# Attention heads of an encoder block: squaring before splitting, scores before q's low part, and small softmax steps on GpSimd

## The chip, the cores and the metric

The kernel runs on one core of a Trainium2 chip. A core has five engines that work side by side and are tied together by semaphores: TensorE (PE in the profile; its weight loads are PEld), VectorE (DVE), ScalarE (ACT), GpSimd (POOL) and SyncE (SP), which here only issues DMAs. Each engine takes its instructions strictly in the order in which the kernel gives them. The metric is the device time of one execution in microseconds (us). Before the change the median of three runs is 946.17 us (945.48 to 946.81).

## The reference

One layer of a bidirectional encoder on 256 tokens of width 2048, in float32:

```python
h = _rmsnorm(x, norm1_g)
proj = h @ w_in                      # q (12 heads x 128) | k, v (4 x 128 each) | u (512)
a = _rmsnorm(_window_attention(q, k, v, sink), attn_out_g)
f = _rmsnorm(_fourier_mix(u, w_fourier), fourier_out_g)
x = x + jnp.concatenate([a, f], axis=-1) @ w_out
x = x + _conv_ffn(_rmsnorm(x, norm2_g), w_up, dw_w, dw_b, w_down)
return _rmsnorm(x, normf_g)
```

Three query heads share one key and value head. The attention of one head, with the parts that the change touches:

```python
scores = einsum(q, k) * HEAD_DIM ** -0.5 - slope * |t - s|      # NEG_INF beyond 128
m = maximum(max(scores), sink)
p = exp(scores - m)
p = p / (sum(p) + exp(sink - m))
out = einsum(p, v)
```

The RMS norm over all heads' outputs needs the sum of their squares.

## The kernel before

**Products in three parts.** Every float32 operand of a matmul is split into a high part (`hi`, the value rounded to the matmul's reduced format) and a low part (`lo`, the rest). A product is hi x hi + lo x hi + hi x lo. ACT makes the high part by a copy (line 181 for weights, line 269 in `split_scaled`), DVE the low part by a subtraction (lines 182 and 270), so the low part always waits for the high one.

**Units.** The weights come in 1 MB units of 128 x 2048. `unit(i, work)` issues, in this order: the steps registered for `before` unit i, the matmuls of the unit, the steps registered `beside` it, the split of the weights of unit i + 2 (ACT `hi`, 1.9 us, then DVE `lo`, 2.3 us), and the steps `behind`. Units 0 to 3 are the projection u, 4 to 7 v, 8 to 23 the four groups k, q, q, q (line 350), 24 to 39 the output projection (lines 333 to 335). From 256 us on comes the feed-forward part, which the change leaves alone.

**A head's way through the units.** The order is written out by hand in the loop over `N_QK` to `N_OUT + 8`. For a q head computed in unit s:

- s + 1, beside: `qk_out` (ACT copies one half of the product out of PSUM as `tmp_q`, DVE adds the other: `add_q`; for k, DVE multiplies by r1b as well, line 635) and `qk_parts` (ACT writes the high part of `qT`, DVE the low part).
- s + 2, before: `scores`, six matmuls on `qT` and `kT` (line 654). For either token block the first two need only `qT`'s high part, the third needs the low part. Beside: `scores_out`, on DVE two fused add-and-maximum passes (line 670), then two instructions of 128 x 2 (lines 674 and 675) that give `neg`, the negated maximum. Behind: `exps`, on ACT, which needs `neg`.
- s + 3, beside: `weigh`, on DVE: the sum `sm` (line 693), its reciprocal (694), two scalings of the probabilities in place (697), and `flip_out`, a block transpose (314) whose result SP sends through memory.
- s + 6, beside: `flip_parts` (lines 739 and 740) splits the transposed probabilities.
- s + 7, before: `values`, six matmuls (line 749); beside: `values_out`, that is `feature_out`: `split_scaled` on the head's output in PSUM (ACT, then DVE), then the square on ACT (line 486 for the first head, 489 for the others), and for all but the first head an addition to `sq_a` on GpSimd (line 490).

The last two heads take a shorter way with a transpose on TensorE. `feature_out` also serves the four Fourier groups, whose outputs lie in SBUF. PSUM is read by one engine at a time: where ACT and DVE both read one tile of PSUM, the second waits for the first, so the square of a head's output waits for DVE's `cat` (line 270).

The pattern repeats every four units. Units 8, 12, 16, 20 compute k. In a unit that follows a k unit (17, 21) the new slot is k; in units 10, 14, 18, 22 there are no scores to take out; in units 11, 15, 19, 23 there is no `weigh` and no `values`.

**Buffers that matter here.** `hi` and `lo` have three buffers each, so a split runs up to two units ahead of its matmuls. `qT`, `mx`, `neg`, `sm` and `ex` have two each, the square's scratch `junk` one.

Of the kernel before, what the change touches and what calls it, by code (L numbers as in the profile page):

```python
# [8 lines left out]
F32 = mybir.dt.float32  # L9
F32R = mybir.dt.float32r  # L10
AF = mybir.ActivationFunctionType
ALU = mybir.AluOpType

P = 128
D = 2048
S = 256
# [88 lines left out]
def block_kernel(  # L105
# [19 lines left out]
    nc = tc.nc  # L125
# [3 lines left out]
    wp = ctx.enter_context(tc.tile_pool(name="wp", bufs=1))  # L129
# [3 lines left out]
    def f32(ap):  # L133
        return ap.bitcast(F32)

    def bank(pool, name):
        return pool.tile([P, 512], F32, tag=pool.name, name=name)
# [79 lines left out]
    def u_part(k, o, n, m=1):  # L217

        rows = ux[k // 4][:, (k < 4) * U_HEAD :].rearrange("p (k c) -> p k c", k=4)
        return rows[:, k % 4 : k % 4 + m, o : o + n]  # L220
# [39 lines left out]
    ps = bank(dn, "ps_warm")  # L260
# [3 lines left out]
    def vcol(o, n=1):  # L264
        return vec[:, o : o + n]

    def split_scaled(dst, src, g):

        nc.scalar.activation(dst[:, 0:S], src, AF.Copy, scale=g)
        nc.vector.scalar_tensor_tensor(  # L270
            dst[:, S : 2 * S], src, g, f32(dst[:, 0:S]), ALU.mult, ALU.subtract
        )
# [100 lines left out]
    before, beside, behind = {}, {}, {}  # L373

    def at(when, i, f, *a):
        when.setdefault(i, []).append((f, a))
# [17 lines left out]
    for k in range(NK):  # L394
# [7 lines left out]
        if q % n == 0:  # L402
            w, h = u_part(k, 0, FW, n), hi[:, q : q + n, :]
# [26 lines left out]
    rq_neg = ph.tile([P, 2], F32, tag="rq_neg", name="rq_neg")  # L430
    rq_pos = ph.tile([P, 2], F32, tag="rq_pos", name="rq_pos")
    rq_inv = ph.tile([P, 2], F32, tag="rq_inv", name="rq_inv")
    sink_neg = ph.tile([P, NH], F32, tag="sink_neg", name="sink_neg")
# [46 lines left out]
    def feature_out(ps, slot, g, sq, first):  # L480

        t = cat_pool.tile([P, 512], F32R, tag="cat", name=f"cat{slot}")
        split_scaled(t, ps, g)
        cat[slot] = t
        if first:
            nc.scalar.activation(sq, ps, AF.Square)
        else:
            one = wp.tile([P, 512], F32, tag="junk", name=f"sq{slot}")[:, 0:S]
            nc.scalar.activation(one, ps, AF.Square)
            nc.gpsimd.tensor_tensor(sq, sq, one, ALU.add)  # L490

    sums, r_af = {}, {}
# [91 lines left out]
    def fourier_channels_out(g):  # L584
        feature_out(held.pop(("y", g)), NH + g, vcol(V_GF + g), sq_f, g == 0)
# [43 lines left out]
    def qk_out(kind, h, ps):  # L629
        tmp = ph.tile([P, S], F32, tag="tmp", name=f"tmp_{kind}{h}", bufs=2)  # L630
        nc.scalar.activation(tmp, ps[:, S : 2 * S], AF.Copy)
        add = ph.tile([P, S], F32, tag="add", name=f"add_{kind}{h}", bufs=2)
        nc.vector.tensor_tensor(add, ps[:, 0:S], tmp, ALU.add)
        if kind == "k":
            nc.vector.tensor_tensor(add, add, r1b, ALU.mult)
        st["add", kind, h] = add
# [25 lines left out]
    def scores_out(h):  # L662

        ps = st.pop(("s", h))
        sc = ph.tile([P, 512], F32, tag="sc", name=f"sc{h}", bufs=4)
        mx = ph.tile([P, 2], F32, tag="mx", name=f"mx{h}", bufs=2)
        neg = ph.tile([P, 2], F32, tag="neg", name=f"neg{h}", bufs=2)
        for b in range(2):
            s = slice(b * S, (b + 1) * S)
            nc.vector.tensor_tensor_reduce(  # L670
                sc[:, s], ps[:, s], rel[:, s], -float(SL[h]), -3e38, ALU.add,
                ALU.max, mx[:, b : b + 1],
            )
        nc.vector.tensor_tensor(neg, mx, rq_neg, ALU.mult)
        nc.vector.tensor_scalar(neg, neg, sink_neg[:, h : h + 1], None, ALU.min)
        st["sc", h] = sc, neg

    def exps(h):
        sc, neg = st["sc", h]
        sm = ph.tile([P, 2], F32, tag="sm", name=f"sm{h}", bufs=2)  # L680
        ex = ph.tile([P, 2], F32, tag="ex", name=f"ex{h}", bufs=2)
        for b in range(2):
            s = slice(b * S, (b + 1) * S)
            nc.scalar.activation(
                sc[:, s], sc[:, s], AF.Exp, scale=rq_pos[:, b : b + 1],
                bias=neg[:, b : b + 1], accum_out=sm[:, b : b + 1],
            )
        nc.scalar.activation(ex, neg, AF.Exp, bias=vcol(V_SINK + h))
        st["sc", h] = sc, sm, ex

    def weigh(h):
        sc, sm, ex = st["sc", h]
        nc.vector.tensor_tensor(sm, sm, ex, ALU.add)
        nc.vector.reciprocal(ex, sm)
        for b in range(2):
            s = slice(b * S, (b + 1) * S)
            nc.vector.tensor_scalar(sc[:, s], sc[:, s], ex[:, b : b + 1], None, ALU.mult)
# [59 lines left out]
    def values_out(h):  # L757
        feature_out(st.pop(("o", h))[:, 0:S], h, vcol(V_GA + h), sq_a, h == 0)
# [3 lines left out]
    for i in range(N_QK, N_OUT + 8):  # L762
        heads = {i - s: h for (kind, h), s in slot_of.items() if kind == "q"}
        new = [kh for kh, s in slot_of.items() if i - s == 1]
        for n, h in sorted(heads.items()):
            if n == 5 + 2 * (h in FLIPS):
                at(before, i, values, h)
        if 4 in heads and heads[4] not in FLIPS:
            at(before, i, turn, heads[4])
        if 2 in heads:  # L770
            at(before, i, scores, heads[2])
        if 6 in heads and heads[6] in FLIPS:
            at(beside, i, flip_parts, heads[6])
        if 3 in heads:
            at(beside, i, weigh, heads[3])
            if heads[3] in FLIPS:
                at(beside, i, flip_out, heads[3])
        if 4 in heads and heads[4] in FLIPS:
            at(beside, i, flip_in, heads[4])
        for kind, h in new:  # L780
            at(beside, i, lambda k=kind, h=h: qk_out(k, h, st.pop(("ps", k, h))))
        for n, h in sorted(heads.items()):
            if n == 5 + 2 * (h in FLIPS):
                at(beside, i, values_out, h)
        if 4 in heads and heads[4] not in FLIPS:
            at(beside, i, turn_out, heads[4])
        for kind, h in new:
            at(beside, i, qk_parts, kind, h)
        if 2 in heads:
            at(beside, i, scores_out, heads[2])  # L790
            at(behind, i, exps, heads[2])

    fourier_channels_steps()
# [84 lines left out]
    for n, (c, kq) in enumerate(OUT_ORDER):  # L878
        i = N_OUT + n
# [14 lines left out]
        if kq >= 2:  # L894
            part = "a" if kq == 2 else "f"
            ps = ps_a[c] if kq < 3 else ps_a[c, "f"]
# [315 lines left out]
    for q in range(2):  # L1212
        kind, j = items[q]
        ps = bank(mm, f"ps_{kind}{j}")
# [15 lines left out]
    for n, it in enumerate(items):  # L1230
# [8 lines left out]
        if it[0] in ("gate", "val"):  # L1239
            kind, j = it  # L1240
            ps = bank(mm, f"ps_{kind}{j}")
# [4 lines left out]
        if it[0] == "product":  # L1246
# [4 lines left out]
            elif end and p in ("P2", "N4"):  # L1251
                ps = joined[c, p] = bank(mm, f"ps_{p}{g}{c}")
                by_parts(ps, parts[p], *halves.pop(it), GROUPS[g][1], True, False)
            else:
                ps = bank(mm, f"ps_{p}{g}{c}")
# [5 lines left out]
        else:  # L1261
            kind, c = it
            hi, lo = halves.pop(up_index[n])
            if c < 2:
                ps = [joined.pop((c, p)) for p in ("P2", "N4")]
            else:
                ps = [bank(mm, f"ps_l{c}{b}") for b in range(2)]
# [10 lines left out]
    i = up_index[n]  # L1278
# [37 lines left out]
    junk = wp.tile([P, 512], F32, tag="junk", name="junkc31")[:, 0:256]  # L1316
# [120 lines left out]
```

## Time and profile before

| what | value |
|---|---|
| median of three runs | 946.17 us (945.48 to 946.81) |
| the profiled execution | 944.83 us, of which the span is 943.0 us |
| TensorE busy | 930.6 us, 99% of the span |
| VectorE busy | 771.4 us, 82% |
| ScalarE busy | 540.5 us, 57% |
| GpSimd busy | 50.8 us, 5%, 68 instructions |
| mean granted TensorE clock | 0.993 |

Times in the profile are microseconds from the start of the span. A line of a timeline gives the start, the duration, the engine, the line of the kernel, the operation, and output <- inputs; what stands in brackets is the idle time of the engine before it and what ended that. Matmuls overlap, so a line's duration is longer than its distance to the next. The profiled execution is 1.34 us shorter than the median.

### The profile page before, as it was taken

How to read it: one execution, taken by the hardware profiler on the slowest of the kernel's cores; microseconds unless marked ns; L12 is line 12 of the kernel's file. 1: busy time of each engine (PE TensorE's matmuls, PEld its weight loads, DVE VectorE, ACT ScalarE, POOL GpSimd, SP SyncE). 2: the span in 40 equal slices, each digit the busy share in tenths (PEclk: the TensorE clock that was granted, in tenths of full speed). 3: DMA queues.
4: the chain of work that ended last, by engine and by line, in shares of the span. 5: the costliest groups of instructions: out<-in, count | busy, mean ns of one | idle time of the engine just before them, and what ended most of it. 6: DMA issues, size and time to landing. Idle time of an engine off the chain costs nothing.

```text
span 943.0 us, 12851 instructions
## 1 busy us (share of the span) xinstructions
PE 930.6 (99%) x5005; PEld 805.6 (85%) x5005; DVE 771.4 (82%) x981; ACT 540.5 (57%) x672; POOL 50.8 (5%) x68
## 2 busy tenths in 40 slices
PE   9999989999999999999999999999999999999996
PEld 7888878888888888888888888888888888888885
DVE  7658788777777878799887997878988779989986
ACT  7755566645554564566555565555655556655553
POOL 0100000100000000000000000000000000000002
PEclk9999989999999999999999999999999999999998
DMA  9965766566766578877798769787787878779652
GB/s 364 310 224 168 225 200 190 191 209 248 259 229 206 183 238 245 269 250 235 250 272 254 243 230 284 241 265 228 260 247 239 301 240 266 226 236 277 201 179 89
DMA packets 55149, 223.26 MB, mean 237 GB/s; under 512 B 21136, under 2 KB 25744, under 8 KB 31536
## 3 DMA queue, kind: packets, MB, share of 16 engines
q1 hardware_dynamic: 50544, 192.94, 56.6%
q0 software_dynamic: 4544, 29.49, 16.7%
q8 instruction: 39, 0.64, 0.3%
q14 instruction: 22, 0.18, 0.1%
HBM read 216.13 MB, written 6.29 MB: 236 GB/s over the span
## 4 chain that ended last, share of the span: by engine, by line
PE 88%; DVE 5%; ACT 4%; issue 2%; DMA 1%; DVEq 0%; SPq 0%; POOLq 0%; POOL 0%; ACTq 0%
PE ps_val L350 25%; PE ps_gate L350 25%; PE ps_P L1148 3%; PE ps_P L1146 3%; PE ps_P L1147 3%; PE ps_N L1148 3%; PE ps_N L1147 3%; PE ps_N L1146 3%; PE ps_a L335 2%; PE ps_a L334 2%; PE ps_a L333 2%; ACT hi L181 2%; DVE lo L182 1%; PE ps_ff L333 1%; PE ps_ff L335 1%
## 5 line engine op out<-in xcount | busy, mean ns | idle before, releaser
L182 DVE TENSOR_TENSOR lo<-raw,hi 128x2048 fp32r<-128x2048 f32 (+1 forms) x129 | 293.4, 2274 | 46.4 <-ACT hi L181 43.7
L181 ACT ACTIVATE hi<-raw 128x2048 fp32r<-128x2048 f32 (+1 forms) x129 | 245.2, 1901 | 34.2 <-PE ps_a L334 14.4
L350 PE MATMUL ps_val<-hU,hi 128*128 128x512 f32 x688 | 236.2, 389 | 0.0
L350 PE MATMUL ps_gate<-hU,hi 128*128 128x512 f32 x688 | 236.2, 389 | 0.0
L350 PE MATMUL ps_val<-hU,lo 128*128 128x256 f32 x688 | 189.9, 276 | 0.0
L350 PE MATMUL ps_gate<-hU,lo 128*128 128x256 f32 x688 | 189.9, 276 | 0.0
L350 PEld LDWEIGHTS ps_gate<-hU,hi 128*128 128x128 f32 x688 | 129.2, 188 | 26.8
L350 PEld LDWEIGHTS ps_val<-hU,hi 128*128 128x128 f32 x688 | 129.1, 188 | 26.8
L350 PEld LDWEIGHTS ps_gate<-hU,lo 128*128 128x128 f32 x688 | 129.2, 188 | 1.3
L350 PEld LDWEIGHTS ps_val<-hU,lo 128*128 128x128 f32 x688 | 129.2, 188 | 1.3
L921 ACT ACTIVATE ft_g<-ps_gate 128x256 f32<-128x256 f32 x43 | 16.5, 384 | 123.1 <-PE ps_gate L350 123.1
L921 ACT ACTIVATE ft_v<-ps_val 128x256 f32<-128x256 f32 x43 | 16.5, 384 | 91.8 <-PE ps_val L350 91.8
L350 PE MATMUL ps_q<-hT,hi 128*128 128x512 f32 x192 | 67.2, 401 | 0.0
L1146 PE MATMUL ps_P<-hi_P,op_P 128*128 128x512 f32 x144 | 56.0, 389 | 0.0
L1147 PE MATMUL ps_P<-hi_P,op_P 128*128 128x512 f32 x144 | 56.0, 389 | 0.0
L1148 PE MATMUL ps_P<-lo_P,op_P 128*128 128x512 f32 x144 | 56.0, 389 | 0.0
L350 PE MATMUL ps_q<-hT,lo 128*128 128x256 f32 x192 | 52.0, 281 | 0.0
L1038 DVE TENSOR_TENSOR lo_N<-sumw,hi_N 128x2048 fp32r<-128x2048 f32 (+1 forms) x20 | 41.5, 2076 | 9.4 <-ACT hi_N L1037 9.2
L350 PEld LDWEIGHTS ps_q<-hT,hi 128*128 128x128 f32 x192 | 36.3, 194 | 7.0
L1146 PE MATMUL ps_N<-hi_N,op_N 128*128 128x512 f32 x108 | 42.0, 389 | 0.0
L1147 PE MATMUL ps_N<-hi_N,op_N 128*128 128x512 f32 x108 | 42.0, 389 | 0.0
L1148 PE MATMUL ps_N<-lo_N,op_N 128*128 128x512 f32 x108 | 42.0, 389 | 0.0
(389 smaller groups left out, 1584.7 us busy)
## 6 DMA issues: line engine op xcount, KB each, us to landing
raw<-in_w_up SPq DMA_DIRECT2D x86, 1024.0 KB, 5.6
raw<-in_w_in SPq DMA_DIRECT2D x20, 1024.0 KB, 5.2
raw<-in_w_out SPq DMA_DIRECT2D x16, 1024.0 KB, 5.0
sumw<-in_w_down POOLq DMA_DIRECT2D x16, 1024.0 KB, 8.7
raw<-in_w_down_late SPq DMA_DIRECT2D x4, 1024.0 KB, 6.9
raw<-in_w_down_last SPq DMA_DIRECT2D x4, 768.0 KB, 4.2
turnp<-flip SPq DMA_DIRECT2D x40, 64.0 KB, 3.0
flop<-turnp SPq DMA_DIRECT2D x10, 256.0 KB, 4.0
```

The costliest lines, as they stand in the source:

```text
L181: nc.scalar.activation(hi[:, 0:n], raw[:, 0:n], AF.Copy)
L182: nc.vector.tensor_tensor(lo[:, 0:n], raw[:, 0:n], f32(hi[:, 0:n]), ALU.subtract)
L333: nc.tensor.matmul(ps, ah, wh, start=first and q == q0, stop=False)
L334: nc.tensor.matmul(ps, al, wh, start=False, stop=False)
L335: nc.tensor.matmul(ps, ah, wl, start=False, stop=last and q == q0 + len(kk) - 1)
L350: nc.tensor.matmul(ps[:, x], (hi, lo)[i][:, k * P : (k + 1) * P], hk(k)[:, x], start=n == 0 and k == 0, stop=n == len(order) - 1 and k == ...
L921: nc.scalar.activation(tmp, ps[:, S : 2 * S], AF.Copy)
L1038: nc.vector.tensor_tensor(lo, src, f32(hi), ALU.subtract)
L1146: nc.tensor.matmul(ps, o[:, 0, p, :], hi[:, s], start=first and p == 0, stop=False)
L1147: nc.tensor.matmul(ps, o[:, 1, p, :], hi[:, s], start=False, stop=False)
L1148: nc.tensor.matmul(ps, o[:, 0, p, :], lo[:, s], start=False, stop=last and p == n - 1)
```

## The change

Three edits.

1. In `feature_out` ACT squares the head's output before it is split, so on ACT the square stands ahead of the high part of `cat`, and it no longer comes after DVE's low part.
2. In each unit `scores_out` is registered ahead of `qk_parts`, so on DVE the two passes of line 670 stand ahead of the low part of the new `qT` or `kT`.
3. Three instructions of 128 x 2 per head move from DVE to GpSimd: lines 674 and 675 (`neg`), and the sum of line 693, which now stands in `exps`, behind the exponentials. `exps` now waits for GpSimd, and the reciprocal of `weigh` as well.

```diff
     def feature_out(ps, slot, g, sq, first):
 
         t = cat_pool.tile([P, 512], F32R, tag="cat", name=f"cat{slot}")
+        one = sq
+        if not first:
+            one = wp.tile([P, 512], F32, tag="junk", name=f"sq{slot}")[:, 0:S]
+        nc.scalar.activation(one, ps, AF.Square)
         split_scaled(t, ps, g)
         cat[slot] = t
-        if first:
-            nc.scalar.activation(sq, ps, AF.Square)
-        else:
-            one = wp.tile([P, 512], F32, tag="junk", name=f"sq{slot}")[:, 0:S]
-            nc.scalar.activation(one, ps, AF.Square)
+        if not first:
             nc.gpsimd.tensor_tensor(sq, sq, one, ALU.add)
...
-        nc.vector.tensor_tensor(neg, mx, rq_neg, ALU.mult)
-        nc.vector.tensor_scalar(neg, neg, sink_neg[:, h : h + 1], None, ALU.min)
+        nc.gpsimd.tensor_tensor(neg, mx, rq_neg, ALU.mult)
+        nc.gpsimd.tensor_scalar(neg, neg, sink_neg[:, h : h + 1], None, ALU.min)
         st["sc", h] = sc, neg
...
         nc.scalar.activation(ex, neg, AF.Exp, bias=vcol(V_SINK + h))
+        nc.gpsimd.tensor_tensor(sm, sm, ex, ALU.add)
         st["sc", h] = sc, sm, ex
...
         sc, sm, ex = st["sc", h]
-        nc.vector.tensor_tensor(sm, sm, ex, ALU.add)
         nc.vector.reciprocal(ex, sm)
...
+        if 2 in heads:
+            at(beside, i, scores_out, heads[2])
         for kind, h in new:
             at(beside, i, qk_parts, kind, h)
         if 2 in heads:
-            at(beside, i, scores_out, heads[2])
             at(behind, i, exps, heads[2])
```

On GpSimd the order of a unit is then: the addition of line 490, the two instructions of `neg`, and, behind the exponentials, the sum. All else keeps its order on every engine; the DMA queues are as before.

## The prediction

> **What bounds the kernel now.** The page first: TensorE is busy for 99% of the span, so a change on other engines can only give back what TensorE waits, and what it loses after a wait. The view of waits, for PE alone, says where that is.
>
> ```profile
> PE 930.6 (99%) x5005; PEld 805.6 (85%) x5005; DVE 771.4 (82%) x981; ACT 540.5 (57%) x672; POOL 50.8 (5%) x68
> ```
>
> ```profile
> PE ps_s L654 <- ACT qT L269: 2.5, 1, 2.5
> ...
> PE ps_s L654 <- DVE qT L270: 0.2, 1, 0.2
> ```
>
> Both waits are scores that come before their q is split. PE's timeline places them: at the start of units 19 and 23.
>
> ```profile
> 95.91 1.20 PE L654 MATMUL ps_s<-kT,qT 128*128 128x256 f32 x6
> ...
> 122.15 0.40 PE L350 MATMUL ps_q<-hT,lo 128*128 128x256 f32 x2
> 125.09 2.01 PE L654 MATMUL ps_s<-kT,qT 128*128 128x256 f32 x6 [2.54 <-ACT qT L269]
> ...
> 134.56 0.40 PE L749 MATMUL ps_o<-pt,v_hi 128*128 128x256 f32 x2
> ...
> 148.34 0.40 PE L749 MATMUL ps_o<-pt,v_hi 128*128 128x256 f32 x2
> ...
> 149.06 0.63 PE L350 MATMUL ps_q<-hT,hi 128*128 128x512 f32 x2
> ...
> 154.54 0.40 PE L654 MATMUL ps_s<-kT,qT 128*128 128x256 f32 x2
> 155.15 0.74 PE L654 MATMUL ps_s<-kT,qT 128*128 128x256 f32 x4 [0.22 <-DVE qT L270]
> 155.74 0.63 PE L350 MATMUL ps_q<-hT,hi 128*128 128x512 f32 x2
> ```
>
> A unit's 32 matmuls take 5.48 us (149.06 to 154.54); units 20 to 22 with all that stands between take 19.98 us (134.56 to 154.54) without a wait. The wait at unit 19 costs more than its 2.54 us, as windows around it show (last columns: granted clock, DMA share, GB/s):
>
> ```profile
> 121.30:124.70 3.40, 1.25 (x8) 0.93 (x7) 2.85 (x8) 0.94 (x4) 0.00 (x0) 1.00 0.50 149
> 124.73:128.15 3.42, 3.06 (x10) 2.59 (x11) 2.03 (x2) 2.99 (x6) 0.72 (x1) 0.50 0.95 300
> 128.15:131.56 3.41, 3.41 (x12) 2.86 (x11) 2.93 (x8) 1.36 (x2) 0.00 (x0) 0.50 0.36 98
> ```
>
> From 124.73 us, 2.18 us after PE fell idle (122.15 + 0.40), until 131.56 the clock is at half: work from 125.09 to 131.56 goes half as fast, which costs 3.24 us. In all unit 19 is some 6 us late. Yet not all of that can be won: by 154 us PE has run into the next wait. The pace there is set by a loop between ACT and DVE, read from their timelines for unit 18 (DVE, then ACT, whose last line is the same step of unit 22):
>
> ```profile
> 118.47 0.41 DVE L670 CUSTOM_DVE_ANT_0 sc<-ps_s,rel 128x256 f32<-128x256 f32 x1
> ...
> 119.27 0.16 DVE L674 TENSOR_TENSOR neg<-mx,rq_neg 128x2 f32<-128x2 f32 x1
> 119.46 0.23 DVE L675 TENSOR_SCALAR neg<-neg,sink_neg 128x2 f32<-128x2 f32 x1
> 119.60 2.29 DVE L182 TENSOR_TENSOR lo<-raw,hi 128x2048 fp32r<-128x2048 f32 x1
> 121.80 0.15 DVE L693 TENSOR_TENSOR sm<-sm,ex 128x2 f32<-128x2 f32 x1
> 121.99 0.17 DVE L694 RECIPROCAL ex<-sm 128x2 f32<-128x2 f32 x1
> 122.19 0.62 DVE L697 TENSOR_SCALAR sc<-sc,ex 128x256 f32<-128x256 f32 x2
> 122.84 0.71 DVE L314 STREAM_TRANSPOSE flip<-sc 128x512 f32<-128x512 f32 x1
> 123.48 0.39 DVE L633 TENSOR_TENSOR add_q<-ps_q,tmp_q 128x256 f32<-128x256 f32 x1
> 123.79 0.47 DVE L270 SCALAR_TENSOR_TENSOR cat<-ps_o,vec,cat 128x256 fp32r<-128x256 f32 x1
> 125.07 0.75 DVE L270 SCALAR_TENSOR_TENSOR qT<-add_q,qT 128x256 fp32r<-128x256 f32 x1 [0.81 <-ACT qT L269]
> ```
>
> ```profile
> 117.65 1.91 ACT L181 ACTIVATE hi<-raw 128x2048 fp32r<-128x2048 f32 x1
> 119.79 0.60 ACT L684 ACTIVATE sc<-sc,neg,rq_pos 128x256 f32<-128x256 f32 x1 [0.23 <-DVE neg L675]
> ...
> 121.16 0.36 ACT L631 ACTIVATE tmp_q<-ps_q 128x256 f32<-128x256 f32 x1
> 121.43 0.46 ACT L269 ACTIVATE cat<-ps_o,vec 128x256 fp32r<-128x256 f32 x1
> 124.35 0.39 ACT L489 ACTIVATE sq<-ps_o 128x256 f32<-128x256 f32 x1 [2.46 <-DVE cat L270]
> 124.63 0.41 ACT L269 ACTIVATE qT<-add_q 128x256 fp32r<-128x256 f32 x1
> 124.94 1.90 ACT L181 ACTIVATE hi<-raw 128x2048 fp32r<-128x2048 f32 x1
> ...
> 154.20 1.91 ACT L181 ACTIVATE hi<-raw 128x2048 fp32r<-128x2048 f32 x1
> ```
>
> Loop: ACT's hi at 117.65, DVE's lo, weigh, flip, add_q, cat, then ACT's sq, qT and the next hi at 124.94. It takes 7.29 us here, and from unit 18 to unit 22 it takes 29.26 us (154.20 − 124.94), where PE's four units would take about 26.2 (19.98 + 5.48 + 0.72 for unit 19 without a wait; 0.72 is values, 148.34 to 149.06, and scores take about the same). So PE gains on the loop by 3 us in every group and meets it at units 19 and 23. After unit 23 PE waits no more, so what is won there stays to the end.
>
> **The change part by part.**
>
> *Square ahead of the split.* The view of waits shows what goes:
>
> ```profile
> ACT sq L489 <- DVE cat L270: 24.9, 11, 3.3
> ```
>
> Unit 18: add_q ends at 123.87, yet qT starts at 124.63, because sq waits for cat's low part. Now sq stands at 121.43, behind tmp_q and ahead of cat's high part, in time in which ACT idled 2.46 us; qT can start at 123.90. That takes 0.73 us off the loop, in each of the units 16, 17, 18, 20, 21, 22 that holds a head's output and precedes the waits. In the Fourier groups the square also comes first, and DVE's cat waits some 0.4 us longer; DVE idles longer than that for the next hi, so this costs nothing:
>
> ```profile
> 70.00 2.29 DVE L182 TENSOR_TENSOR lo<-raw,hi 128x2048 fp32r<-128x2048 f32 x1 [1.89 <-ACT hi L181]
> ```
>
> *Line 490 on GpSimd comes earlier with it,* and what it meets changes.
>
> ```profile
> 124.81 0.72 POOL L490 TENSOR_TENSOR sq_a<-sq_a,sq 128x256 f32<-128x256 f32 x1 [6.55 <-ACT sq L489]
> ```
>
> ```profile
> 130.65 0.42 DVE L270 SCALAR_TENSOR_TENSOR qT<-add_q,qT 128x256 fp32r<-128x256 f32 x1 [0.48 <-ACT qT L269]
> ```
>
> The qT step that begins at 125.07 beside this addition takes 0.75 instead of 0.42 us, and ends 0.29 us after the addition does: DVE was held. There it delays scores, not the loop. After the change the addition is ready at 121.82, while DVE's lo runs, and would lie at about 122.0 to 122.74, beside the reciprocal and the scaling of line 697. No row shows whether that scaling is held. If not: 0. If held until the addition ends, it finishes at about 122.9 instead of 122.5, or 0.35 us later; a subtraction of line 740 in its place (units 17, 20, 21) could lose 0.6. I take 0.33, nearest the row that shows a hold. The Trainium skill, page "SBUF — State Buffer", section "Who interferes with whom", says that DVE's two-input and two-port instructions and GpSimd exclude each other for a whole instruction, whichever comes first blocking the other, and counts tensor_scalar among those that can take two ports. The row above agrees for GpSimd coming first; by this rule the 0.33 is due, and the gain of the first edit nearly halves.
>
> *Three small steps to GpSimd.* DVE loses 0.20 + 0.14 (119.27 to 119.60) and 0.19 us (121.80). The first two were beside ACT's hi and gain little. GpSimd's nearest rows: 0.19 us for a small addition, 0.70 for a power.
>
> ```profile
> L280 POOL TENSOR_TENSOR rstda<-vara,half_pow 128x2 f32<-128x2 f32 x1 | 0.7, 702 | 7.3 <-DVE vara L277 7.3
> ...
> L1323 POOL TENSOR_TENSOR ssq<-ssq 128x1 f32<-128x1 f32 x2 | 0.4, 192 | 1.2 <-ACT junkc L1165 0.9 <-ACT junkc L1317 0.3
> ```
>
> I take 0.2 each. sm is ready once the exponentials end at 121.16. If GpSimd runs it at once, the reciprocal follows lo directly: −0.19. If lo holds it until 121.80, sm ends at 122.0 and the reciprocal stays where it was, at worst 0.05 later. I take 0, and +0.1 for the heads before unit 15, where no head's output is there to gain on: the scores at 95.91 start 0.1 us later. For neg, the exponentials must not wait: priced as a rival.
>
> *Scores ahead of qT's low part.* DVE fills its idle 0.81 us before qT's low part with four instructions of 0.80 us (118.47 to 119.27). Behind them waits the low part, which the third score matmul needs: against the loop it ends up to 0.4 us later in units 16, 20 and 24, so the scores of the unit after could come to wait; the bounds are 0 and 0.4 each, 0.8 ahead of unit 23. Units 18 and 22, which feed the two waits, hold no scores_out, so I take 0. No DMA and no queue is moved.
>
> *Sum.* Loop starts of hi: unit 18 at 124.94 + 0.1 − 0.73 (unit 16, whose first head adds nothing on GpSimd) − 2 × 0.40 = 123.5. PE, at 122.65, finds qT's high part at 123.6: it waits 0.9 us instead of 2.54, too short, I take it, for the clock to fall. Unit 22's hi: 154.20 + 0.1 − 0.73 − 5 × 0.40 = 151.6. In unit 23 before, q's matmuls began 1.54 us after that hi, of which 0.33 was a hold of qT by the addition, as at 125.07, that is now gone: 152.8 against 155.74, 2.95 us earlier. PE itself arrives in time: unit 19 ends at 123.5 + 1.2 + 5.48 = 130.2, unit 22 at 150.2, so it waits about 1.4 us at unit 23, again without a fall. I round to 3.0 us: 944.83 − 3.0 = 941.8 for an execution like the profiled one, which was 1.34 below the median, so **943.2** as a median.
>
> **The rivals.**
>
> *The clock falls at the wait of unit 23.* PE is ahead of the loop now, and the wait grows from 0.22 us, at which the clock stayed, to 1.4; before, 2.18 us idle sufficed. A fall costs what it cost then, 3.24 us, and takes the gain: 944.83 − 3.0 + 3.2 = 945.0, 946.4 as a median. (A fall at unit 19 instead would mostly be absorbed at unit 23: PE would arrive there 3.24 later, 153.4, plus 0.7 for scores, so gain 1.6.) The Trainium skill, "TensorE: Matmul & The Clock Gate", Part 1, lets the clock fall after a window of about 3.4 us of idling; by that neither wait would do it, but here 2.18 us did, so the row decides.
>
> *Nothing holds anything.* Six units save 0.73 + 0.19: hi of unit 22 at 148.7, PE no longer waits at unit 19 nor, to speak of, at 23, and of its losses of 6.0 and 0.5 some 6 come back: 944.83 − 6.0 = 938.8, median 940.2.
>
> *The holds eat it.* 0.6 for line 740, 0.05 for sm and an added 0.1 leave nothing: 946.2.
>
> *Slower: neg falls behind the split's lo.* The passes of line 670 now end about 0.78 us after ACT's hi begins (add_q to hi 0.73; cat 0.31 + 0.40 and 0.80 after add_q), qT's low part 0.34 later, and DVE's lo begins 1.95 after it (117.65 to 119.60). Held behind qT, the two GpSimd steps start at 1.12 and need 0.4 to 0.5: done by 1.6, slack 0.35. At 0.70 each they still get in, the second at 1.85, and lo loses 0.5. If the second starts after 1.95 and lo holds it to 4.15, the exponentials (1.37 us, 119.79 to 121.16) end at 5.8, the reciprocal moves from 4.34 to 6.0, 1.65 us per unit. Six units: 9.9 lost against 3.0, 944.83 + 6.9 = 951.7, median 953.1.
>
> **How the numbers follow.** Chances: the forecast 0.48 (own range 941.5 to 944.5), the clock falls 0.20, nothing holds 0.12, holds eat it 0.10, slower 0.10. The range 940.2 to 947.6 takes in the free case, the fallen clock and the eaten gain, and leaves out the last. This kernel can tell 0.2%, 1.9 us, from no change: faster means below 944.3, the forecast almost wholly and the free case, 0.57 with the forecast's upper edge taken off; within are the fallen clock, the eaten gain and that edge, 0.31; slower 0.12, the last case and a clock that falls at both waits.
>
> **What would show it.** Right: no wait of sq on cat; qT 0.03 us behind add_q; unit 19's wait near 0.9 us at full clock, unit 23's near 1.4; scalings of line 697 longer than 0.35 us beside line 490; line 689 held until lo ends; exponentials directly behind hi. Wrong: half clock near 150 us; neg later than lo's start; PE's waits elsewhere than at units 19 and 23.

## The result, and the profile after

The changed kernel takes 941.28 us (median; 940.97 to 941.60) against 946.39 us (945.48 to 946.81) for the kernel before in the same comparison. The ratio is 0.995, with a 95% interval of 0.9936 to 0.9964: faster by 0.54%. In a second comparison (the last row of the table below) the ratio was 0.9955 (0.9943 to 0.9967). The forecast was a gain of 3.0 us to 943.2; the gain is 5.1 us in the first comparison and 4.0 in the second. The profiled executions, 944.83 and 941.03 us, differ by 3.8.

The page's line of busy times and the view of PE's waits, of the changed kernel:

```profile
PE 928.0 (99%) x5005; PEld 803.5 (86%) x5005; DVE 765.5 (82%) x945; ACT 539.6 (57%) x672; POOL 72.9 (8%) x104
```

```profile
PE ps_s L654 <- ACT qT L269: 1.4, 2, 0.9
```

The two waits lie where they lay before, at the starts of units 19 and 23 (PE's timeline of the changed kernel; the last row is the start of q's matmuls of unit 23):

```profile
122.94 1.19 PE L654 MATMUL ps_s<-kT,qT 128*128 128x256 f32 x6 [0.54 <-ACT qT L269]
...
150.43 1.20 PE L654 MATMUL ps_s<-kT,qT 128*128 128x256 f32 x6 [0.85 <-ACT qT L269]
151.47 0.61 PE L350 MATMUL ps_q<-hT,hi 128*128 128x512 f32 x2
```

They were 2.54 and 0.22 us. q's matmuls of unit 23 start at 151.47 instead of 155.74 us. The table by windows gives the same from PE's side: busy time of each engine from 110 to 160 us, then granted clock, DMA share and GB/s, first of the kernel before, then of the changed one:

```profile
110.00:160.00 50.00, 47.24 (x273) 41.78 (x272) 41.42 (x93) 30.51 (x67) 3.68 (x5) 0.93 0.63 187
```

```profile
110.00:160.00 50.00, 48.60 (x299) 43.16 (x298) 41.15 (x79) 32.76 (x76) 12.91 (x21) 1.00 0.69 210
```

In the same 50 us PE issues 26 more matmuls: it is busy for 1.36 us more, as its waits are shorter, and the clock stays full (1.00 instead of 0.93). The view of waits has no row of sq on cat any more. This is the loop of unit 18 in the changed kernel, DVE, ACT and GpSimd, to be held against the timelines in the prediction:

```profile
117.93 2.29 DVE L182 TENSOR_TENSOR lo<-raw,hi 128x2048 fp32r<-128x2048 f32 x1 [0.87 <-ACT hi L181]
120.31 0.17 DVE L694 RECIPROCAL ex<-sm 128x2 f32<-128x2 f32 x1
120.51 0.86 DVE L697 TENSOR_SCALAR sc<-sc,ex 128x256 f32<-128x256 f32 x2
121.41 0.71 DVE L314 STREAM_TRANSPOSE flip<-sc 128x512 f32<-128x512 f32 x1
122.05 0.39 DVE L633 TENSOR_TENSOR add_q<-ps_q,tmp_q 128x256 f32<-128x256 f32 x1
```

```profile
116.00 1.90 ACT L181 ACTIVATE hi<-raw 128x2048 fp32r<-128x2048 f32 x1
...
119.42 0.37 ACT L486 ACTIVATE sq<-ps_o 128x256 f32<-128x256 f32 x1
119.69 0.46 ACT L269 ACTIVATE cat<-ps_o,vec 128x256 fp32r<-128x256 f32 x1
122.47 0.42 ACT L269 ACTIVATE qT<-add_q 128x256 fp32r<-128x256 f32 x1 [2.32 <-DVE add_q L633]
122.79 1.90 ACT L181 ACTIVATE hi<-raw 128x2048 fp32r<-128x2048 f32 x1
```

```profile
116.80 0.31 POOL L674 TENSOR_TENSOR neg<-mx,rq_neg 128x2 f32<-128x2 f32 x1 [3.09 <-DVE mx L670]
117.21 0.28 POOL L675 TENSOR_SCALAR neg<-neg,sink_neg 128x2 f32<-128x2 f32 x1
119.33 0.94 POOL L689 TENSOR_TENSOR sm<-sm,ex 128x2 f32<-128x2 f32 x1 [1.84 <-ACT ex L688]
120.24 0.72 POOL L490 TENSOR_TENSOR sq_a<-sq_a,sq 128x256 f32<-128x256 f32 x1
```

The loop takes 6.79 us (116.00 to 122.79) where it took 7.29. From add_q to the next hi it is 0.74 instead of 1.46 us, the square's 0.72. From the reciprocal to the flip it is 1.10 instead of 0.85, since the scaling pair takes 0.86 instead of 0.62 beside line 490. GpSimd's sum of 128 x 2, line 689, takes 0.94 us: it ends at 120.27, 0.05 after DVE's lo, so the reciprocal starts 2.38 us behind lo's start, as before (2.39).

In units 16, 17, 20 and 21, DVE's line 740 stands between lo and the reciprocal, and there the sum does pay. Unit 17, DVE of the kernel before, then of the changed one:

```profile
111.17 2.29 DVE L182 TENSOR_TENSOR lo<-raw,hi 128x2048 fp32r<-128x2048 f32 x1 [0.24 <-ACT hi L181]
113.38 0.76 DVE L740 TENSOR_TENSOR pt<-flop,pt 128x256 fp32r<-128x256 f32 x2
114.05 0.15 DVE L693 TENSOR_TENSOR sm<-sm,ex 128x2 f32<-128x2 f32 x1
114.24 0.17 DVE L694 RECIPROCAL ex<-sm 128x2 f32<-128x2 f32 x1
```

```profile
110.15 2.30 DVE L182 TENSOR_TENSOR lo<-raw,hi 128x2048 fp32r<-128x2048 f32 x1 [0.88 <-ACT hi L181]
112.36 0.76 DVE L740 TENSOR_TENSOR pt<-flop,pt 128x256 fp32r<-128x256 f32 x2
113.03 0.16 DVE L694 RECIPROCAL ex<-sm 128x2 f32<-128x2 f32 x1
113.23 0.90 DVE L697 TENSOR_SCALAR sc<-sc,ex 128x256 f32<-128x256 f32 x2
```

Lo's start to the reciprocal: 3.07 before, 2.88 after, all of the sum's 0.19. Line 740 itself is not held (0.76 both times).

### The profile page after: what moved, and what is told of

It reads as the page before. It is cut to its first block, busy times and chain, and to the rows that moved or that the text cites. A ratio compares the mean times of both kernels' runs of the same rounds, so it can differ in the third digit from the quotient of the medians.

```text
span 938.9 us, 12849 instructions
## 1 busy us (share of the span) xinstructions
PE 928.0 (99%) x5005; PEld 803.5 (86%) x5005; DVE 765.5 (82%) x945; ACT 539.6 (57%) x672; POOL 72.9 (8%) x104
## 4 chain that ended last, share of the span: by engine, by line
PE 95%; DVE 2%; ACT 1%; issue 1%; DMA 0%; POOL 0%; DVEq 0%; POOLq 0%; ACTq 0%
PE ps_val L350 25%; PE ps_gate L350 25%; PE ps_q L350 5%; PE ps_P L1148 3%; PE ps_P L1149 3%; PE ps_P L1147 3%; PE ps_N L1148 3%; PE ps_N L1149 3%; PE ps_N L1147 3%; PE ps_k L350 2%; PE ps_a L333 2%; PE ps_a L335 2%; PE ps_a L334 2%; PE ps_s L654 1%; PE ps_ff L333 1%; PE ps_ff L335 1%
## 5 line engine op out<-in xcount | busy, mean ns | idle before, releaser
L350 PE MATMUL ps_q<-hT,hi 128*128 128x512 f32 x192 | 65.1, 391 | 0.0
```

Source lines behind the costliest of these rows:

```text
L350: nc.tensor.matmul(ps[:, x], (hi, lo)[i][:, k * P : (k + 1) * P], hk(k)[:, x], start=n == 0 and k == 0, stop=n == len(order) - 1 and k == ...
```

## The experiments

The theory after the comparison: the time follows the ACT and DVE loop of units 16 to 22, and each edit counts by what it takes from that loop; the square gives, the addition on GpSimd takes some of it back, and the scores' place does nothing. Rivals: the gain is the full clock alone; or it is the 0.5 us per head that DVE no longer does.

**The kernel before, again.** 

> The kernel before, unchanged, for a second profile. Is the length of the half clock after the wait of unit 19 fixed? If the clock is looked at in windows of 3.41 us that run freely (6.83 us of half clock in the first profile are two of them), the start of the half clock relative to the wait differs here, and its length is a whole number of 3.41 us; the time of the execution goes with it by 1.7 us per window. If the length is fixed by the wait, start and length repeat within 0.1 us. Time 945.5 to 946.8 us.

945.59 us beside 945.64, ratio 0.9998 (0.9989 to 1.0007). Its profiled execution (945.78 us) has the half clock for 3.4 us only (126.16 to 129.57 us), not the 6.83 of the execution that the prediction used. It starts 2.93 us after PE fell idle instead of 2.18, so start and length are not fixed by the wait, as expected of free windows. That the time goes with it by 1.7 us did not come: from unit 15's hi to the first matmul of the output projection it is 61.28 us here (102.03 to 163.31) and 61.30 in the other execution (101.34 to 162.64). So the loop, not the clock, set the time: what the clock leaves at unit 19, PE waits at unit 23, as the prediction said in brackets. There the wait for qT's high part is 0.93 us, where the other execution waited 0.22 us in all:

```profile
155.05 0.50 PE L654 MATMUL ps_s<-kT,qT 128*128 128x256 f32 x2 [0.93 <-ACT qT L269]
```

**The first edit alone.**

```diff
+        one = sq
+        if not first:
+            one = wp.tile([P, 512], F32, tag="junk", name=f"sq{slot}")[:, 0:S]
+        nc.scalar.activation(one, ps, AF.Square)
         split_scaled(t, ps, g)
         cat[slot] = t
-        if first:
-            nc.scalar.activation(sq, ps, AF.Square)
-        else:
...
+        if not first:
             nc.gpsimd.tensor_tensor(sq, sq, one, ALU.add)
```

> The first edit alone: the square ahead of the split, all else as before. Loop theory (what counts is the time from one ACT hi to the next in units 16 to 22, because PE meets that loop at units 19 and 23): each of six units loses 0.73 us of waiting and, beside line 490, gets back about 0.28 us of a held scaling (none in unit 16): hi of unit 22 at 154.20 - 0.73 - 5 x 0.45 = 151.2, about 3 us less in all, 943 to 943.5 us; no half clock at unit 19. Load theory (what counts is work taken off VectorE): no VectorE instruction goes, so 946 us, no change.

943.29 us, ratio 0.9976 (0.9966 to 0.9985): the time is in the expected range, with 2.35 us gained where about 3 was expected. The way there was not as expected, so the range was met in part by luck: from unit 15 to unit 22 the loop gave 1.55 us (52.86 to 51.31 between the hi's), not 2.98. Unit 18's gave 0.19 us, not 0.73 less a small hold: the sum of line 693, still on DVE, is now held by GpSimd's addition (GpSimd's timeline, then DVE's, then a window around unit 19):

```profile
120.60 0.94 POOL L490 TENSOR_TENSOR sq_a<-sq_a,sq 128x256 f32<-128x256 f32 x1 [6.62 <-ACT sq L486]
```

```profile
120.88 0.69 DVE L693 TENSOR_TENSOR sm<-sm,ex 128x2 f32<-128x2 f32 x1
...
121.81 0.61 DVE L697 TENSOR_SCALAR sc<-sc,ex 128x256 f32<-128x256 f32 x2
```

```profile
124.80:128.20 3.40, 3.40 (x14) 2.91 (x13) 2.44 (x2) 1.81 (x4) 0.00 (x0) 0.50 0.73 183
```

0.69 us for an instruction that took 0.15: 0.54 of the 0.73 is lost there. And no half clock was expected, yet the clock fell after a wait of 1.55 us.

**The second edit alone.**

```diff
+        if 2 in heads:
+            at(beside, i, scores_out, heads[2])
         for kind, h in new:
             at(beside, i, qk_parts, kind, h)
         if 2 in heads:
-            at(beside, i, scores_out, heads[2])
             at(behind, i, exps, heads[2])
```

> The second edit alone: lines 670 to 675 ahead of the low part of qT or kT on VectorE, all else as before. Loop theory: DVE's next lo waits for ACT's hi in any case, and hi waits for sq and qT, which do not move: no change, 945.5 to 946.8 us, the stall of unit 19 as before with half clock. Load theory: 0.8 us of VectorE's idle time is filled in nine units, some 3 us or more less: 943 us.

945.28 us, ratio 0.9999 (0.999 to 1.0008): nothing, and the loop from unit 15 to 22 is unchanged (52.88 us). The clock was not as expected: in the profiled execution (946.72 us) it stays full after the wait of 2.54 us at unit 19 and falls after one of 2.21 us at unit 23, for one stretch of 3.4 us. From unit 22's hi to the output projection it then takes 9.71 us (154.58 to 164.29) where the kernel before takes 8.44, and no later wait makes up for that.

**The third edit alone.**

```diff
-        nc.vector.tensor_tensor(neg, mx, rq_neg, ALU.mult)
-        nc.vector.tensor_scalar(neg, neg, sink_neg[:, h : h + 1], None, ALU.min)
+        nc.gpsimd.tensor_tensor(neg, mx, rq_neg, ALU.mult)
+        nc.gpsimd.tensor_scalar(neg, neg, sink_neg[:, h : h + 1], None, ALU.min)
...
+        nc.gpsimd.tensor_tensor(sm, sm, ex, ALU.add)
...
-        nc.vector.tensor_tensor(sm, sm, ex, ALU.add)
```

> The third edit alone: three small steps per head on GpSimd, all else as before. Loop theory: without the second edit line 670 ends 1.5 to 1.6 us after ACT's hi begins in the units 16, 17, 20, 21, so that GpSimd's second step starts at or after DVE's lo (1.95) and is held until lo ends: neg some 2.2 us late, the exponentials with it, the next reciprocal 1.7 us later in the unit after. Three or more of such holds before unit 23 against 0.19 us saved in units with line 740: slower, 949 to 952 us. Load theory: about 0.55 us of VectorE work less per head, twelve heads, 6.5 us: 940 to 943 us.

951.69 us, ratio 1.0064 (1.0051 to 1.0076): slower by 6.05 us, though DVE does less. Unit 18, GpSimd, DVE (its first row is the low part of the new kT) and ACT:

```profile
119.07 0.20 POOL L674 TENSOR_TENSOR neg<-mx,rq_neg 128x2 f32<-128x2 f32 x1 [1.05 <-DVE mx L670]
119.36 2.43 POOL L675 TENSOR_SCALAR neg<-neg,sink_neg 128x2 f32<-128x2 f32 x1
```

```profile
117.55 0.76 DVE L644 TENSOR_TENSOR kT<-add_k,kT 128x256 fp32r<-128x256 f32 x1 [0.76 <-ACT kT L643]
...
119.35 2.29 DVE L182 TENSOR_TENSOR lo<-raw,hi 128x2048 fp32r<-128x2048 f32 x1 [0.36 <-ACT hi L181]
123.60 0.17 DVE L694 RECIPROCAL ex<-sm 128x2 f32<-128x2 f32 x1 [1.96 <-POOL sm L689]
```

```profile
121.83 0.60 ACT L684 ACTIVATE sc<-sc,neg,rq_pos 128x256 f32<-128x256 f32 x1 [2.51 <-POOL neg L675]
```

The second small step comes 0.01 us behind lo's start and takes 2.43 us, until lo has ended at 121.64; the exponentials and the reciprocal come late, and the loop takes 9.07 us (hi at 117.41 and 126.48), 1.78 more than before. That is the mechanism of the prediction's slower rival, priced there at 1.65. It happens in the loops of units 18, 21 and 22, where line 490 lies beside the low part of qT or kT ahead of line 670 and makes it 0.76 us long; in those of units 16, 17 and 20 that low part takes 0.42 to 0.43 us, and neg is in time. Three holds make the loop from unit 15 to 22 4.67 us longer (57.53 against 52.86). At unit 23 PE then waits 4.02 us, and the clock is at half from 158.55 to 165.38 us:

```profile
159.24 2.01 PE L654 MATMUL ps_s<-kT,qT 128*128 128x256 f32 x6 [4.02 <-ACT qT L269]
```

From unit 22's hi to the output projection it takes 10.91 us instead of 8.44, so some 2.5 of the 7.4 us that this execution has lost by there are the clock's. That the time comes near the price of that rival (951.7 us for an execution, 953.1 as a median), which stood on six holds and no fall, is chance. The run also does away with the rival of DVE's load: the edit that takes 36 instructions from DVE costs 6 us by itself.

**Two edits at a time, and all three again.** The diffs are those above, put together.

> The first and second edits, without the steps on GpSimd. Loop theory: as the first edit alone (943.3), since the second is not on the loop: 943.0 to 943.6 us. Load theory: half-way between the first edit alone and all three, 942.3 us.

> The first and third edits, without the scores ahead of q's low part. Loop theory: with the square gone from ahead of qT, qT's low part no longer waits, line 670 ends about 1.3 us after ACT's hi begins, and GpSimd's second step starts at about 1.7, before DVE's lo at 1.95: neg comes in time, and all that the three edits give is there: 941.0 to 942.0 us. Rival: neg is still held in some units, as in the third edit alone (951.7): 944 us or more.

> The second and third edits, without the square ahead. Loop theory: line 670 ends about when ACT's hi begins, so neg is in time and nothing of the 6 us that the third edit loses alone remains; 0.19 us is saved in the units with line 740 (16, 17, 20, 21) and in unit 12: about 0.95 us, 944.4 to 945.2 us. Rival (the loss of the third edit alone came from GpSimd's slower steps as such, not from a hold): still 950 us.

> The changed kernel, unchanged, timed beside the pairs of edits. 940.9 to 941.6 us; waits of 0.5 and 0.9 us at units 19 and 23 at full clock, as in its first profile.

| edits | median us | ratio to before, interval |
|---|---|---|
| 1 and 2 | 943.75 | 0.9983 (0.9974 to 0.9991) |
| 1 and 3 | 941.01 | 0.995 (0.9938 to 0.9962) |
| 2 and 3 | 944.11 | 0.9985 (0.9976 to 0.9994) |
| all | 941.39 | 0.9955 (0.9943 to 0.9967) |

The edits do not add up: 1 alone gives 2.35 us, 3 alone costs 6.05, both together give 4.4. Either of edits 1 and 2 brings neg in ahead of lo. The second does so by putting line 670 earlier on DVE; with 2 and 3, neg is there 0.6 us ahead of lo (GpSimd, and DVE's lo, of unit 18):

```profile
117.77 0.28 POOL L675 TENSOR_SCALAR neg<-neg,sink_neg 128x2 f32<-128x2 f32 x1
```

```profile
118.66 2.29 DVE L182 TENSOR_TENSOR lo<-raw,hi 128x2048 fp32r<-128x2048 f32 x1 [1.05 <-ACT hi L181]
```

The first does so by moving line 490: its addition no longer lies beside the low part of qT or kT. With 1 and 3 that step of unit 18 takes 0.42 us again, not 0.76, and the second small step starts 1.61 us after ACT's hi instead of 1.95 (117.55 and 115.94, against 119.36 and 117.41):

```profile
116.06 0.42 DVE L644 TENSOR_TENSOR kT<-add_k,kT 128x256 fp32r<-128x256 f32 x1
```

With edit 1 there, the second is not needed. 1 and 2 came out just above the expectation (943.0 to 943.6). 2 and 3 came out a little below theirs (944.4 to 945.2): unit 22's hi comes 1.64 us earlier than before (152.56 against 154.20), where 0.95 was expected. The profiled execution (944.56 us) loses 1.58 us of that again from there to the output projection, for the clock falls after a wait of 1.69 us at unit 23.

**Without the additions on GpSimd.** In the changed kernel:

```diff
-        if not first:
+        if not first and slot >= NH:
             nc.gpsimd.tensor_tensor(sq, sq, one, ALU.add)
```

> The changed kernel without the additions of line 490 for the heads (the sum of squares holds the first head alone, so the attention group is scaled wrongly; the Fourier groups keep theirs). If the addition holds DVE's scaling of line 697 by 0.28 us in each of the units 17, 18, 20, 21, 22, the pair takes 0.62 us again, hi of unit 22 comes 1.4 us earlier, the waits of units 19 and 23 shrink to nearly nothing: 1.0 to 1.4 us less, 939.9 to 940.4 us. Rival (the two waits are set by something else): 941.2 us.

939.93 us, ratio 0.9941 (0.9929 to 0.9954), beside 945.22 for the kernel before: 1.35 us below the changed kernel's 941.28, and 0.9 to 1.3 us below it by the two ratios of that kernel. The scaling of unit 18 is short again:

```profile
120.13 0.62 DVE L697 TENSOR_SCALAR sc<-sc,ex 128x256 f32<-128x256 f32 x2
```

The hi of unit 22 starts at 148.83 instead of 150.28, 1.45 earlier, near 5 units of 0.24 to 0.28. The hold is real, and this is all that it costs.

**The new q or k ahead of the softmax, on top of all three edits.** If PE's two waits are set by the loop, the sum of line 633 can be made to come ahead of the reciprocal, the scaling and the flip:

```diff
+        for kind, h in new:
+            at(beside, i, lambda k=kind, h=h: qk_out(k, h, st.pop(("ps", k, h))))
         if 6 in heads and heads[6] in FLIPS:
             at(beside, i, flip_parts, heads[6])
...
-        for kind, h in new:
-            at(beside, i, lambda k=kind, h=h: qk_out(k, h, st.pop(("ps", k, h))))
```

> The changed kernel with qk_out moved to the front of the steps beside a unit, ahead of flip_parts and weigh. That shortens the loop from hi to hi to about 5 us, below PE's 6.5 per unit, so that no wait at units 19 and 23 should be left: 939 us, if neg is in time. But hi then ends long before DVE is through line 670, and DVE's next lo follows qT's low part without a gap, so GpSimd's second step of neg should be held for all of lo in every unit with scores, 2.2 us, and ACT's exponentials and all behind them with it, a chain of about 8 us per unit: 948 to 955 us. Load theory makes no difference to the changed kernel: 941 us.

941.32 us, ratio 0.9958 (0.9946 to 0.9971): the mechanism came, the loss did not. Neg is held in the loops of units 14, 17, 18, 21 and 22, as here (GpSimd, then DVE, unit 18):

```profile
117.55 2.20 POOL L675 TENSOR_SCALAR neg<-neg,sink_neg 128x2 f32<-128x2 f32 x1
```

```profile
117.32 2.28 DVE L182 TENSOR_TENSOR lo<-raw,hi 128x2048 fp32r<-128x2048 f32 x1
```

The loop takes 8.49 us there (hi at 113.85 and 122.34), but the next takes 5.01 (to 127.35), so four units come to 27.45 us (122.34 to 149.79), near the 27.49 of the changed kernel (122.79 to 150.28). I had priced every unit as a held one.

**The same with the small steps on DVE** (the kernel before, edits 1 and 2, and the diff above). 

> The same with the three small steps back on VectorE (first and second edits, and qk_out first). No hold of neg; VectorE's work per four units is about 25 us against PE's 26.2. PE waits at no scores: 938.8 to 939.8 us, faster than both kernels. Rival (VectorE cannot do without the relief of GpSimd): 942 us or more, waits at scores again.

938.12 us (938.05 to 939.10), ratio 0.9926 (0.9913 to 0.994): 0.7 us below the expected range, faster than either kernel and 3.2 us below the one above. The view of PE's waits has one row left, and it lies in the warm-up:

```profile
PE ps_warm L262 <- POOL ones L254: 1.0, 1, 1.0
```

```profile
117.22 0.42 DVE L633 TENSOR_TENSOR add_q<-ps_q,tmp_q 128x256 f32<-128x256 f32 x1
117.56 0.41 DVE L693 TENSOR_TENSOR sm<-sm,ex 128x2 f32<-128x2 f32 x1
...
118.20 0.61 DVE L697 TENSOR_SCALAR sc<-sc,ex 128x256 f32<-128x256 f32 x2
```

```profile
118.00 1.90 ACT L181 ACTIVATE hi<-raw 128x2048 fp32r<-128x2048 f32 x1
122.16 0.39 ACT L631 ACTIVATE tmp_q<-ps_q 128x256 f32<-128x256 f32 x1 [2.26 <-PE ps_q L350]
```

Unit 18's next hi comes at 118.00, 4.79 earlier than in the changed kernel, and ACT now waits for PE (2.26 us for q's matmuls): PE has become the bound of these units. The small steps on DVE cost nothing there. How much the order does without edits 1 and 2 was not tried.

## Why the prediction was right, and where its sizes were off

*What bounds the kernel:* right. PE's waits stayed at units 19 and 23, and almost nothing is lost after unit 23: q's matmuls there come 4.27 us earlier, the span ends 4.1 earlier (943.0 and 938.9), and the profiled execution, which has 1.8 us outside its span before and 2.1 after, ends 3.8 earlier. That half clock at unit 19 costs little by itself was right too (the kernel before, again).

*Square ahead of the split, 0.73 per unit:* right where its cover was right: 0.72 in unit 18, 0.65 in unit 16 (add_q to hi). By itself it would have lost most of that again, which the prediction did not see: the first edit alone gives 0.19 in unit 18, since the addition then meets line 693. It pays because the third edit takes that instruction out of the way.

*Line 490 on GpSimd, 0.33 per unit:* right as a mechanism, a little too dear: 0.24 in unit 18 (0.86 against 0.62) and 0.28 in unit 17 (0.90). The 0.6 of line 740 does not occur. The rule of the Trainium skill, page "SBUF — State Buffer", section "Who interferes with whom", that the engine that comes first keeps the other out, agrees with these rows in both directions: the addition lengthens the scaling, and a GpSimd step that takes 0.28 us when free takes 2.43 behind lo.

*Three small steps to GpSimd, sm at 0 and +0.1 before unit 15:* this is the step that was mis-sized. The sum is held until lo ends, as said, but in units 16, 17, 20 and 21 line 740 comes next on DVE, so the reciprocal gains 0.19 in each. Before unit 15 the hi comes 0.17 earlier (101.17 against 101.34), not 0.1 later.

*Scores ahead of q's low part, 0:* right alone (0.9999). With the third edit but without the first it is worth 7.35 us (1.30 faster than before instead of 6.05 slower, each beside its own runs of the kernel before), mostly since it brings neg in ahead of lo: the loop from unit 15 to 22 is 5.85 us shorter (51.68 against 57.53), and the half clock at unit 23 lasts one stretch instead of two. In the sum it stands at nothing because the first edit does that already.

*The sum:* the loop gave up 3.75 us from unit 15 to unit 22 (52.86 to 49.11 between the hi's) where 2.73 was forecast, and with 0.17 instead of −0.1 ahead of it 3.92 against 2.63. The 1.29 between them is 0.76 from sm, some 0.35 from smaller holds, 0.27 before unit 15, less 0.08 for unit 16's square. The waits are 0.54 and 0.85 us instead of 0.9 and 1.4, without a fall, as forecast. The other part of the miss is the 1.34 us that was added for an execution below its median: in the changed kernel it is 0.25. Both made the forecast too slow, and 941.28 lies just below the 941.5 to 944.5 that the prediction gave its own case.

*The rivals:* that nothing holds anything is excluded by the run without additions, which gives about 1.3 us more; that the holds eat the gain, by their 0.24 to 0.28. The clock did not fall, as the waits stayed at 0.54 and 0.85 us; that a fall at unit 23 would have stayed to the end is shown by edit 2 alone and by edits 2 and 3, where one stretch cost 1.27 and 1.58 us. The slower case is the third edit alone; in the changed kernel it was near, as GpSimd's line 675 ends 0.44 us before lo starts (117.49 and 117.93), and in one unit it happens. Unit 25, GpSimd, then DVE:

```profile
170.50 2.18 POOL L674 TENSOR_TENSOR neg<-mx,rq_neg 128x2 f32<-128x2 f32 x1 [2.17 <-DVE mx L670]
```

```profile
170.34 2.29 DVE L182 TENSOR_TENSOR lo<-raw,hi 128x2048 fp32r<-128x2048 f32 x1
174.87 0.17 DVE L694 RECIPROCAL ex<-sm 128x2 f32<-128x2 f32 x1 [2.24 <-POOL sm L689]
```

PE waits for nothing there, so it costs nothing.

## What to carry to other kernels

Work taken from a busy engine is worth what it takes from the loop that ends in the bounding engine's next wait: here the edit that took 36 instructions from DVE cost 6 us alone, and the fastest version left them there and put the sum that PE waits for first. A short step on GpSimd must be placed by what DVE begins just before it, because it can wait for the whole of that; look at both queues at the moment it becomes ready. Edits that touch the same loop have to be run alone and in pairs before one of them is credited: in this change the third edit is of use only behind one of the others.

## What the runs showed of the hardware

DVE's instructions with two inputs in SBUF (lo, line 693, the low part of qT or kT) and its scaling, and GpSimd's steps, keep each other out in these rows, in either order, until the one that came first has ended; the reciprocal is not held (0.17 us beside line 490 in unit 18). A GpSimd step of 128 x 2 takes 0.19 to 0.31 us when free, and 2.18 to 2.44 when it starts with lo or just behind it; a DVE addition of 128 x 2 takes 0.15 us when free and 0.69 beside GpSimd's addition of 128 x 256; the low part of qT or kT takes 0.42 and 0.76; the scaling pair takes 0.62 and 0.86 to 0.90.

The clock fell after shorter waits than I had thought, and not after every longer one: after 1.55 us (the first edit alone), 1.69 and 2.21 us (unit 23 with edits 2 and 3, and with edit 2 alone), but not after 2.00 and 2.54 us at unit 19 in those same two runs, nor after 1.53 us at either unit with edits 1 and 2; in both executions of the kernel before it fell after 2.54 us. It stays down for one or two stretches of 3.41 us. Falls of one execution lie on one grid: with the third edit alone they begin at 127.83 and 158.55 us, nine stretches apart. If that grid is carried through each execution, PE was busy for 0.08 to 1.86 us of the 3.41 just before a fall, and for 1.75 us or more of those without one. So by an estimate from these busy times a wait counts by the share of one window that it fills, and about half is enough: the 2.54 us of edit 2 alone fell on two windows (2.12 and 1.88 us busy). As 1.75 to 1.88 us lie on both sides, the exact share stays open. The Trainium skill, page "TensorE: Matmul & The Clock Gate", Part 1, has the clock follow free-running windows of about 3.4 us and fall after one that was idle. The length and the grid agree; that the whole window must be idle does not, at a wait of 1.55 us.
